# A scan's scaled old states no longer count in the estimate that places its next matmuls

## The chip, the cores and the metric

The kernel runs on one core of a Trainium2 chip. The core has five engines with queues of their own, each worked off strictly in the order in which the program was written: TensorE (PE, matmuls), VectorE (DVE), ScalarE (ACT), GpSimd (POOL) and SyncE (SP, which only issues DMAs; ACT issues some too). The metric is the device time of one execution in microseconds (us), the median of several runs. Lower is better.

## The reference

One encoder layer is applied to two request groups with one set of weights: group 0 has 512 tokens, group 1 has 1024. The kernel treats them as three blocks of 512 (b = 0 and 1 belong to group 1, b = 2 to group 0).

```python
x = x + 0.5 * mod[2] * rmsnorm(swiglu(h, f1_w1, f1_w3, f1_w2), n1_post)   # feed-forward 1
z = modulate(rmsnorm(x, nm_pre), ...) @ w_in                               # projections
m = concat([pool_mixer(z[..., :512]), rwkv7_mixer(token_shift(z[..., 512:]))])
x = x + mod[5] * rmsnorm(m @ w_out, nm_post)
x = x + 0.5 * mod[8] * rmsnorm(swiglu(h, f2_w1, f2_w3, f2_w2), n2_post)   # feed-forward 2
# in rwkv7_mixer, for each of 8 heads and both directions, token by token:
S = S * w_t + (S @ na_t) b_t^T + v_t k_t^T
y = S @ r_t
```

## The kernel before, in words

**Two kinds of work on PE.** The feed-forwards and projections are matmuls of 128x128 by 128x512 on split operands (each product is three of them: high by high, low by high, high by low). They are called wide matmuls here; there are 11520, written in a fixed sequence, and "wide matmul 6384" is the 6384th of them. They write the tiles u, v and y from hh, hl, gh, gl (split activations) and whi, wlo (split weights; whi is an ACT copy, wlo a subtraction on POOL or, while the scan runs, on DVE). All other matmuls are narrow; most belong to the scan.

**The scan.** The recurrence is done in chunks of 64 tokens. Eight pairs of heads (four of group 1, then four of group 0), each with all chunks in groups of four, give 24 groups and 96 steps. For a group, `scan_prep` loads and builds the operands (AR, BKt, MU), `scan_inv` inverts a triangular matrix per chunk (tile XN; even groups on DVE, odd ones on POOL; one inversion at a time), `scan_state` makes the four steps, and `scan_post` normalises the output (tile yT) and stores it to DRAM (m). A step of `scan_state` has two directions and these stages:

1. W: matmuls from the old state SBD and from MU into PSUM (tile sb), copied by ACT to a piece of XN (`wsb`, so the trace shows XN<-sb);
2. ACT scales the old states by a decay into s0p, two instructions per step, left out at the first and the last step of a pair (160 in all);
3. U: matmuls of XN and MU, copied by ACT (MU<-sb);
4. matmuls with BKt for the new state and with AR for the output, and on DVE the new state SBD <- sb, PL, s0p.

**What sets the order.** All parts are Python generators. While the program is written, `run_until` always continues one of them, and so decides which instructions come next in every engine's queue. It does so by an estimate: `Estimate.op` adds up assumed costs per engine, and keeps in `est.last` when the latest result written since a generator was continued would be there. At `yield WAIT` the generator becomes ready again at that time plus a lead (200 ns for the scan's steps, which have priority 0):

```python
elif r == CHAIN:
    p_.ready = est.last - CHAIN_LEAD
else:
    p_.ready = max(est.last + (AFTER_STATE if p_.prio == 0 else AFTER_OTHER), est.free["T"] + (0.0 if r == WAIT else r))
```

Until then the other generators, the main program (`mainC`) above all, put their matmuls into PE's queue. None of this is a wait on the chip; there, PE takes its queue in order, and each instruction waits for its own operands by semaphores.

**The main program around the scan** runs, in wide matmuls: feed-forward 1 of block 2 (up to 5712), pooled half of the output projection for block 0 (to 5808), the projections z of group 0 (to 6288), the pooled half for block 1 (to 6384), the other half for block 0, `wout_gen(0)` (to 6480), which needs the scan's output of all of group 1 and loads it with `mload_gen`, the pooled half for block 2 (to 6576), then feed-forward 2. The projections of group 0 begin with a norm of block 2, and feed-forward 2 of block 0 with a norm of what `wout_gen(0)` gave. A stretch in which no wide matmul stands because the main program cannot go on is called a hole here.

## Time and profile before

| what | value |
|---|---|
| median of 3 runs | 3704.02 us (3702.42 to 3704.77) |
| the profiled execution: its time | 3696.6 us |
| its span, first to last instruction | 3694.9 us |
| mean granted PE clock | 0.957 |
| PE, DVE, ACT, POOL busy | 94%, 54%, 39%, 38% of the span |
| first and last U matmul of the scan | 1258.4 and 2617.2 us |

A row of the page or of a view names line, engine, operation and tiles as out<-in. Every instruction of this kernel is recorded at one helper line (L161), so tiles tell what it is: sb and XN, MU, s0p, SBD belong to the scan's steps, sM to its other parts. A group has its count, its busy time in us and the mean in ns; a row of waits has the total in us, the times and the longest; a row of a timeline has start and length in us and, in brackets, the idle time before it and what ended it; a row of windows has length, then busy time (and instructions) of PE, weight load, DVE, ACT and POOL, the granted clock, the DMA share and GB/s.

### The profile page before, as it was taken

What the parts mean: (1) busy time and instruction counts of PE and PEld (TensorE: products, weight loads), DVE (VectorE), ACT (ScalarE), POOL (GpSimd) and SP (SyncE); (2) the same over time, 40 slices, a digit from 0 to 9 for tenths busy, and PEclk for the clock granted to TensorE, in tenths of its full rate; (3) what the DMA queues carried; (4) which work ended last, traced back from release to release, by engine and by line L of the source; (5) the groups of instructions that cost most, each with busy time, mean ns of one, the idle gap of its engine ahead of it and who ended that gap; (6) DMA issues with size and microseconds to landing.
All of it is one profiled execution on the core that took longest, in us unless ns stands there. A gap on an engine that the chain in (4) does not pass through costs nothing. (4 is left out here: it accounts for less than half of the span.)

```text
span 3694.9 us, 53680 instructions
## 1 busy us (share of the span) xinstructions
PE 3489.5 (94%) x19579; PEld 2639.9 (71%) x19579; DVE 2009.6 (54%) x3813; ACT 1436.3 (39%) x2776; POOL 1408.9 (38%) x1705
## 2 busy tenths in 40 slices
PE   7999999998999999999889989899999999999998
PEld 4667878886677666666666666567777788877886
DVE  3118272227326878777886888877467612241224
ACT  3324252224344444444444444543333432233222
POOL 2433444443123322333433234433354344444444
PEclk8999999998999999999978988799999999999999
DMA  7656353334334323223333344222354433343332
GB/s 280 221 182 185 99 151 91 98 92 125 121 123 138 92 82 92 69 78 95 109 100 102 113 144 126 81 86 72 109 177 129 117 100 95 94 123 117 99 91 79
DMA packets 557979, 432.10 MB, mean 117 GB/s; under 512 B 27029, under 2 KB 511572, under 8 KB 553620
## 3 DMA queue, kind: packets, MB, share of 16 engines
q1 hardware_dynamic: 524900, 379.90, 33.6%
q10 hardware_dynamic: 32816, 48.78, 4.2%
q8 instruction: 154, 2.52, 0.3%
q14 instruction: 109, 0.89, 0.1%
HBM read 367.23 MB, written 61.34 MB: 116 GB/s over the span
## 5 line engine op out<-in xcount | busy, mean ns | idle before, releaser
L161 POOL TENSOR_TENSOR wlo<-wraw,whi 128x512 fp32r<-128x512 f32 x670 | 888.0, 1343 | 1294.3 <-ACT whi L161 794.8
L161 DVE TENSOR_TENSOR y<-y,y 128x512 f32<-128x512 f32 x480 | 328.1, 685 | 866.2 <-PE y L161 865.0
L161 ACT ACTIVATE whi<-wraw 128x512 fp32r<-128x512 f32 x938 | 559.0, 622 | 186.3 <-PE v L161 141.5
L161 PE MATMUL u<-hh,whi 128*128 128x512 f32 x1392 | 567.5, 408 | 17.7 <-ACT hh L161 8.5
L161 PE MATMUL u<-hl,whi 128*128 128x512 f32 x1392 | 564.6, 406 | 14.1 <-DVE hl L161 14.0
L161 PE MATMUL v<-hh,whi 128*128 128x512 f32 x1392 | 562.8, 404 | 10.5 <-ACT hh L161 5.5
L161 PE MATMUL u<-hh,wlo 128*128 128x512 f32 x1392 | 566.4, 407 | 0.9 <-DVE wlo L161 0.6
L161 PE MATMUL v<-hl,whi 128*128 128x512 f32 x1392 | 563.0, 404 | 1.7 <-DVE hl L161 1.0
L161 PE MATMUL v<-hh,wlo 128*128 128x512 f32 x1392 | 561.6, 403 | 0.0
L161 PE MATMUL y<-gh,whi 128*128 128x512 f32 x1056 | 425.5, 403 | 12.3 <-DVE y L161 11.3
L161 PE MATMUL y<-gh,wlo 128*128 128x512 f32 x1056 | 422.2, 400 | 0.4 <-DVE wlo L161 0.4
L161 PE MATMUL y<-gl,whi 128*128 128x512 f32 x1056 | 422.5, 400 | 0.0
L161 POOL TENSOR_TENSOR XN<-XN 64x126 f32<-64x126 f32 (+22 forms) x744 | 335.3, 451 | 210.6 <-DVE XN L161 109.1
L161 PEld LDWEIGHTS u<-hh,whi 128*128 128x128 f32 x1392 | 266.3, 191 | 90.2 <-ACT hh L161 12.9
L161 PEld LDWEIGHTS u<-hl,whi 128*128 128x128 f32 x1392 | 266.5, 191 | 82.1 <-DVE hl L161 20.7
L161 ACT ACTIVATE gh<-s 128x512 fp32r<-128x512 f32 x132 | 83.3, 631 | 613.8 <-DVE s L161 613.4
L161 PEld LDWEIGHTS v<-hh,whi 128*128 128x128 f32 x1392 | 265.2, 191 | 79.1 <-ACT hh L161 9.4
L161 PEld LDWEIGHTS u<-hh,wlo 128*128 128x128 f32 x1392 | 266.9, 192 | 71.4 <-issue 10.9
L161 PEld LDWEIGHTS v<-hl,whi 128*128 128x128 f32 x1392 | 265.3, 191 | 68.9 <-issue 5.4
L161 PEld LDWEIGHTS v<-hh,wlo 128*128 128x128 f32 x1392 | 265.4, 191 | 63.5 <-issue 6.2
L161 PEld LDWEIGHTS y<-gh,whi 128*128 128x128 f32 x1056 | 200.9, 190 | 66.2 <-DVE y L161 14.8
L161 PEld LDWEIGHTS y<-gh,wlo 128*128 128x128 f32 x1056 | 200.7, 190 | 48.7 <-issue 3.2
(252 smaller groups left out, 4303.8 us busy)
## 6 DMA issues: line engine op xcount, KB each, us to landing
wraw<-in_f_w_dram SPq DMA_DIRECT2D x792, 256.0 KB
ada<-in_ada_w_dram SPq DMA_DIRECT2D x32, 1024.0 KB
wraw<-in_w_in_dram SPq DMA_DIRECT2D x98, 256.0 KB
xk<-xs ACTq DMA_DIRECT2D x96, 256.0 KB
xs<-y ACTq DMA_DIRECT2D x48, 256.0 KB
wraw<-in_w_out_dram SPq DMA_DIRECT2D x48, 256.0 KB
in_k<-zk SPq DMA_DIRECT2D x48, 128.0 KB
in_kk<-zkk SPq DMA_DIRECT2D x48, 128.0 KB
```

The costliest lines, as they stand in the source:

```text
L161: return f(*args, **kw)
```

## The change

`est.last` is saved before the two scalings of the old states and put back after them. The scalings are still issued, at the same place in ACT's queue, and their assumed cost still counts for ACT; only the time at which the step's generator becomes ready again no longer includes them.

```diff
                 for d in both:
                     S.activation(wsb[d], Wp[d], AF.Copy)
                 if not zero and not lastc:
+                    last = est.last
                     for d in both:
                         s0p[d] = st_(sb, [P, P], f"s0p{d}")
                         S.activation(s0p[d], old[:, d, :], AF.Copy, scale=PL[:, m % 2, gi, d, c:c + 1])
+                    est.last = last
                 yield WAIT
                 for h in both:
                     for d in both:
                         mm(Up[d][:, hl_(h)], MA[0:64, us(d, h), :], wsb[d][:, hl_(h)])
```

Every decision after the first such step can come out differently, so the whole order behind it is another one. The counts of PE's matmuls and of the DMAs are the same; 20 of the weights' low halves (wlo) go from DVE to POOL, since the scan ends earlier in the sequence. Its last matmul stands behind wide matmul 7214 before, and behind 6973 now.

PE at the second step of the scan that has scalings: from the end of W (sb<-MU) to U (sb<-XN,MU). Before:

```order
L161 MATMUL sb_9082<-MU_9075 64x64
L161 MATMUL y_9967<-gh_9576,wlo_9862 128x512
L161 MATMUL v_9928<-hh_8856,whi_9860 128x512
L161 MATMUL v_9928<-hl_8857,whi_9860 128x512
L161 MATMUL v_9928<-hh_8856,wlo_9924 128x512
L161 MATMUL v_9928<-hh_8856,whi_9860 128x512
L161 MATMUL v_9928<-hl_8857,whi_9860 128x512
L161 MATMUL v_9928<-hh_8856,wlo_9924 128x512
L161 MATMUL v_9928<-hh_8856,whi_9860 128x512
L161 MATMUL sb_9081<-XN_9076,MU_9075 64x64
L161 MATMUL sb_9082<-XN_9076,MU_9075 64x64
```

And with the change:

```order
L161 MATMUL sb_9082<-MU_9075 64x64
L161 MATMUL y_9967<-gh_9576,wlo_9862 128x512
L161 MATMUL v_9928<-hh_8856,whi_9860 128x512
L161 MATMUL v_9928<-hl_8857,whi_9860 128x512
L161 MATMUL v_9928<-hh_8856,wlo_9924 128x512
L161 MATMUL sb_9081<-XN_9076,MU_9075 64x64
L161 MATMUL sb_9082<-XN_9076,MU_9075 64x64
```

U stands four wide matmuls earlier.

SP around the end of the pooled half for block 1: wp_181 are its eight stores, one per column, m_177 and m_178 are the scan's last output of group 1 (from yT), and y<-wp opens `wout_gen(0)`. Before:

```order
L161 DMA wp_181<-gh_19272 128x512
L161 DMA wraw_19279<-in_w_out_dram 128x4x128
L161 DMA in_wa_19299<-zw_163 64x256 x2
L161 DMA in_wa_19299<-za_164 64x256 x2
L161 DMA in_k_19304<-zk_160 128x256 x2
L161 DMA in_kk_19307<-zkk_162 128x256 x2
L161 DMA in_r_19310<-zr_159 128x256 x2
L161 DMA wp_181<-gl_19346 128x512
L161 DMA m_177<-yT_17219 128x256
L161 DMA m_178<-yT_17219 128x256
L161 DMA y_19538<-wp_180 128x512 x8
```

And with the change (the eight wp_181 stores follow, and then y<-wp):

```order
L161 DMA m_179<-s_19149 128x512
L161 DMA m_177<-yT_17040 128x256
L161 DMA m_178<-yT_17040 128x256
L161 DMA wraw_19211<-in_w_out_dram 128x4x128
L161 DMA m_179<-s_19243 128x512
L161 DMA m_179<-s_19361 128x512
L161 DMA wp_181<-gh_19377 128x512
L161 DMA wraw_19384<-in_w_out_dram 128x4x128
L161 DMA wp_181<-gl_19452 128x512
```

The last store of the scan's group 1 stands behind the eighth column's store before, and ahead of the first one's now.

## The prediction

> **What bounds the kernel now.** I read the page first: its engine shares and its slices.

> ```profile
> span 3694.9 us, 53680 instructions
> PE 3489.5 (94%) x19579; PEld 2639.9 (71%) x19579; DVE 2009.6 (54%) x3813; ACT 1436.3 (39%) x2776; POOL 1408.9 (38%) x1705
> PE   7999999998999999999889989899999999999998
> PEclk8999999998999999999978988799999999999999
> ```

> The two rows of digits are 40 equal slices of 92 us: TensorE (PE) is busy nearly everywhere, and its granted clock sags in the second half of the scan (slices 21 to 26), where its busy share sags too. The chain of waits on the page does not reach back to the scan, so stages have to be compared by windows: the scan's first part, the middle, its end, and all that follows it.

> ```profile
> 1204.00:1815.00 611.00, 575.84 (x4410) 415.69 (x4409) 485.93 (x1083) 267.45 (x591) 186.23 (x364) 0.96 0.28 84
> 1815.00:2380.00 565.00, 504.42 (x3682) 355.22 (x3679) 449.24 (x994) 267.08 (x589) 230.97 (x415) 0.85 0.38 117
> 2380.00:2622.00 242.00, 232.88 (x1918) 169.18 (x1917) 172.60 (x391) 105.28 (x245) 69.03 (x140) 0.99 0.25 74
> 2622.00:3695.00 1073.00, 1033.34 (x4535) 834.23 (x4533) 415.93 (x609) 357.79 (x627) 477.70 (x362) 0.99 0.38 112
> ```

> Columns: length, then busy time of PE, weight load, DVE, ACT, POOL, then granted clock. I call lost the idle time of PE plus its busy time times (1 - clock): 58 us in the first part, 136 in the middle, 11 at the end, 50 in the 1073 us after the scan. So PE bounds, and the only stage with much to win or lose is the middle of the scan. What PE waits for, over the whole span:

> ```profile
> PE sM L161 <- DVE MU L161: 37.1, 23, 4.2
> PE sb L161 <- DVE SBD L161: 18.6, 32, 2.2
> ...
> PE sb L161 <- ACT XN L161: 1.9, 4, 1.0
> ```

> The last row is the one that the change touches: U matmuls (sb<-XN,MU) waiting for ACT's copies of W (XN<-sb) cost 1.9 us in all. The next step's W waits on the state (SBD), and the inverse's matmuls on DVE (MU), cost more, and the change leaves both alone.

> **The change part by part.** No instruction is added or removed on PE; 160 scalings stay on ACT where they were, behind the two copies. Only places move: PE's U matmuls come forward. One step of the scan in the trace:

> ```profile
> 1710.16 0.45 PE L161 MATMUL sb<-MU 64*64 64x64 f32 x8
> 1710.54 0.50 PE L161 MATMUL y<-gh,whi 128*128 128x512 f32 x1
> 1710.68 0.57 ACT L161 ACTIVATE XN<-sb 64x128 f32<-64x128 f32 x2 [0.78 <-ACT Pt L161]
> 1711.15 0.68 ACT L161 ACTIVATE s0p<-SBD,PL 128x128 f32<-128x128 f32 x2
> 1712.71 0.39 PE L161 MATMUL v<-hh,whi 128*128 128x512 f32 x1
> 1713.03 0.45 PE L161 MATMUL sb<-XN,MU 64*64 64x64 f32 x8
> 3252.28 5.60 PE v L161 x24
> ```

> The copies end at 1711.25 and U starts at 1713.03: 1.78 us in which PE is never idle, because wide matmuls of the main program fill it. A wide matmul takes 5.60/24 = 0.233 us (last row, from the chain after the scan). In the order the commonest number of wide matmuls between W and U falls from 8 to 4, and over 96 steps from 674 to 431. The 243 are not saved, they run elsewhere: 0.233 x 243 = 57 us of cover that the scan no longer uses. **By itself that is 0 us**, since PE does the same work. The rest of the sum is what happens to lost time.

> *(1) The wait for the scan at the first output projection goes: -9 us.* The wide matmuls stop dead for 24 us at number 6384, and the trace says why:

> ```profile
> 2194.95 0.39 PE L161 MATMUL u<-hh,wlo 128*128 128x512 f32 x1
> 2202.18 1.91 PE L161 MATMUL sM<-MU 32*32 32x32 f32 x32 [2.19 <-DVE MU L161]
> 2207.95 1.27 POOL L161 TENSOR_TENSOR yT<-yT,pg 128x512 f32<-128x512 f32 x1
> 2209.25 0.80 SPq L161 DMA_DIRECT2D m<-yT  x2
> 2210.86 0.33 ACTq L161 DMA_DIRECT2D xk<-m  x1
> 2218.54 0.61 ACT L161 ACTIVATE hh<-xk 128x512 fp32r<-128x512 f32 x1
> 2219.21 0.79 PE L161 MATMUL u<-hh,whi 128*128 128x512 f32 x1 [0.23 <-ACT hh L161]
> 2195.00:2219.30 24.30, 18.34 (x183) 13.51 (x181) 16.05 (x34) 9.81 (x25) 9.79 (x23) 0.62 0.54 181
> 2219.30:2246.00 26.70, 26.15 (x160) 17.43 (x160) 17.36 (x34) 8.84 (x23) 22.18 (x45) 0.71 0.22 62
> ```

> The last piece of the scan's output for the first request group is only finished by POOL at 2209.22, stored, loaded back (xk), split (hh), and then the projection starts. In the new order that store lies eight projection columns earlier, so the scan is no longer what is waited for; the load itself still is, because it is requested only when the matmuls before it are written into the order: 2219.21 - 2210.86 = 8.4 us. Work in the hole at full clock is 18.34 x 0.62 = 11.4 us, so 12.9 are lost. Afterwards 34 of the 94 narrow matmuls stand there, 11.4 x 34/94 = 4.1 us, so 8.4 - 4.1 = 4.3 are lost. Difference 8.6, taken as 9. Bounds: -13 (nothing lost) to 0 (another wait takes its place).

> *(2) The slow clock behind that hole: -2 us.* The row 2219.30:2246.00 loses 26.15 x 0.29 = 7.6 us. Shorter holes are followed by a slow clock too (the 8.2 us hole below stands at 0.74), so I take a quarter. Bounds -8 to 0. [...]

> *(3) U waits for the copies: +5 us.* With 4 wide matmuls U would start about 1 us after W, and ACT's copies need 0.71 us (1710.54 to 1711.25): 0.2 to 0.3 us of margin. ACT is busy (267.45 + 267.08 + 105.28)/1418 = 45% of the scan, mostly with pieces like this:

> ```profile
> L161 ACT ACTIVATE whi<-wraw 128x512 fp32r<-128x512 f32 x938 | 559.0, 622 | 186.3 <-PE v L161 141.5
> L161 ACT ACTIVATE s0p<-SBD,PL x160: 385/390/403, 1267.7 to 2610.1; 128x128 f32<-128x128 f32 x160
> ```

> A copy that comes behind one is late by 0 to 0.62 us evenly; less 0.2 of margin that is 0.42 x 0.42/(2 x 0.62) = 0.14 us on average, times 0.45, times the 80 steps that have scalings: 5 us. Behind U on PE stand wide matmuls, which then wait for nothing but lose that time. Bounds: 0 to 80 x 4 x 0.233 = 75 us (each step loses all that it gained), and the first is far nearer, as 1.9 us are lost now. The scalings take 0.39 us each and end at 1711.83 in the step above, before the copies of U are wanted at about 1712.5, so they move no wait.

> *(4) Scan work moves into the second set of projections: -6 us.* Between wide matmuls 5808 and 6288 the order holds 20 U steps where it held 16, and the 251 wide matmuls up to the scan's old end (6963 to 7214) hold one U step where there were nine. Those projections wait for their own finishing work:

> ```profile
> 1874.30:2135.30 261.00, 243.42 (x1721) 170.59 (x1722) 194.94 (x448) 125.83 (x274) 87.65 (x184) 0.88 0.33 98
> 2135.30:2143.50 8.20, 4.05 (x50) 3.16 (x48) 7.56 (x21) 1.83 (x4) 0.70 (x1) 0.74 0.80 243
> ```

> Here 261.0 - 243.4 = 17.6 us are idle, and moved work can fill some of that. I take a third. Bounds -18 to 0.

> *(5) Norms crowded on DVE: +3 us.* From the first to the eighth scaling of the norm that the next feed-forward waits for (at 6576), DVE has 62 instructions in the new order against 27, since an inversion now falls there.

> ```profile
> 2301.10:2339.20 38.10, 28.18 (x251) 22.19 (x249) 32.39 (x68) 16.41 (x37) 10.77 (x8) 0.62 0.41 134
> 2339.15 0.80 PE L161 MATMUL u<-hh,whi 128*128 128x512 f32 x1 [4.03 <-ACT hh L161]
> L161 DVE TENSOR_TENSOR XN<-XN x744: 156/256/1419, 1209.5 to 2529.6; 64x126 f32<-64x126 f32 x18, 64x30 f32<-64x30 f32 x12, 64x56 f32<-64x56 f32 x12, 64x78 f32<-64x78 f32 x12
> 1864.20:1874.30 10.10, 4.30 (x51) 3.43 (x49) 8.55 (x25) 2.73 (x5) 1.95 (x5) 0.77 0.54 156
> ```

> DVE is 32.39/38.10 = 85% busy in that hole, so instructions put there count: 35 x 0.256 = 9 us. Against it the norm before this one is broadcast at wide matmul 6501 instead of 6528: 27 x 0.233 = 6 us earlier. Net +3. The hole at 5808 (last row) gets more of both, waits and work, and I leave it at 0. Bounds 0 to +18 with both holes.

> Sum: -9 - 2 + 5 - 6 + 3 = -9 us. The profiled execution took 3696.6 us (span 3694.9), so 3688 for it; it lay 7 us under the median of 3704.0, against which I forecast **3695**.

> **The rivals.** *Nothing is left (3704).* The hole at 6384 keeps its length because another wait takes over, and the filled idle time returns elsewhere. For it: in the scan's first part, step 40 stands at wide matmul 5711 instead of 5722, that is, the inverses and not the steps set the pace there. Against it: the store visibly moves.

> *Slower: the inversion sits in front of the norm (3718).* Its place is the hole at 6576: DVE does the 35 extra instructions (9 us) before the norm is through, nothing comes earlier for it, and the first 24 wide matmuls behind it run at half clock (24 x 0.233 = 6 us more); the hole at 5808, which must hold 78 narrow matmuls instead of 28, grows by 50 x 11.4/94 = 6 us. That is 21 on top of the sum without (5), -12: +9, and with (3) twice as large +14. It decides from the point where the hole at 6576 is over 50 us long. For it: the 85% of DVE. Against: less scan work of PE stands in that hole, 58 narrow matmuls instead of 132.

> *A larger gain (3681).* (1) and (2) at their far bounds and (4) at -10: -13 - 8 + 5 - 10 + 3 = -23. For it: the middle of the scan loses 136 us, and removing one hole may spare a slow clock that follows it. Against: four other holes stay.

> *Short waits lower the clock (3721).* If 80 short waits more take the scan's clock down by 0.02, that is 1313 us of PE busy time x 0.02 = 26 us on top of the forecast. [...]

> **How the numbers follow.** A measurement of this kernel tells about 0.2%, 7.4 us, from no change, so faster means under 3696.6 and slower over 3711.4. Chances: forecast 0.36 (3689 to 3700; 0.28 of it under the bound), nothing left 0.22, larger gain 0.17, norm slower 0.18, clock 0.07. Faster 0.28 + 0.17 = 0.45; within 0.08 + 0.22 = 0.30; slower 0.18 + 0.07 = 0.25. Range 3671 to 3721: down to -33, near the sum of the far bounds of (1), (2) and (4) with (3) and (5) as taken (-13 - 8 - 18 + 5 + 3 = -31), up to +17, which takes in the norm case. The forecast's own range is 3689 to 3700.

> **What would show it.** (1): between the wide matmuls 6384 and 6385 no more than 12 us, begun by the load xk and not by the store m<-yT. (3): the wait of sb on ACT XN rises from 1.9 us to 4 to 10. (4): idle in the second projections under 17 us. (5): the hole at 6576 between 35 and 48 us. The last U of the scan near 2560 us instead of 2617. The prediction is wrong if the hole at 6384 keeps 20 us or more, if waits on XN pass 15 us, or if the clock in the scan's first part falls under 0.94.

## The result and the profile after

The changed kernel takes 3717.6 us (median of 6 runs, 3712.7 to 3731.2) against 3701.8 us of the kernel before on the same chip. The ratio is **1.0051, with an interval of 1.0035 to 1.0067**: slower by half a per cent, 16 us by the two medians and 19 us by the ratio. The forecast was 3695, a small gain; the measured time is inside the range and on the other side of no change.

The page of the kernel after, its span, the row of PE, and the slices of PE and of its granted clock:

```profile
span 3723.8 us, 53718 instructions
PE 3518.8 (94%) x19579; PEld 2664.9 (72%) x19579; DVE 1988.0 (53%) x3789; ACT 1434.3 (39%) x2774; POOL 1431.2 (38%) x1729
PE   7999999998999999999889989799999999999998
PEclk8999999998999989999969888799999999999999
```

The profiled execution took 3725.65 us, 8 us over its median, and the one before 3696.6 us, 5 us under its own; so the two profiles lie some 13 us further apart than the medians. Span less busy time gives PE's idle time: 3723.8 - 3518.8 = 205.0 us, and 3694.9 - 3489.5 = 205.4 before. **PE waits no longer than before.** The same 19579 matmuls are busy for 29.3 us more, and the span is 28.9 us longer. So the whole difference of the two profiles is a slower clock: the clock records hold 402.6 us at half clock, against 318.6 before.

The four windows of the prediction, in the kernel after (the last one ends with its span):

```profile
1204.00:1815.00 611.00, 581.56 (x4368) 420.99 (x4367) 475.07 (x1075) 265.10 (x587) 181.78 (x362) 0.93 0.28 83
1815.00:2380.00 565.00, 505.15 (x3771) 354.81 (x3769) 447.18 (x997) 258.93 (x587) 227.79 (x418) 0.84 0.37 115
2380.00:2622.00 242.00, 225.74 (x1743) 163.84 (x1742) 165.76 (x381) 107.79 (x240) 86.15 (x152) 0.91 0.25 74
2622.00:3722.00 1100.00, 1062.90 (x4659) 859.18 (x4657) 414.03 (x599) 363.69 (x636) 490.78 (x374) 0.99 0.37 111
```

The clock went from 0.96, 0.85 and 0.99 to 0.93, 0.84 and 0.91 in the first three of these windows; behind the scan nothing changed. And PE's longest waits in the scan:

```profile
PE sM L161 <- DVE MU L161: 25.1, 19, 3.6
PE sb L161 <- DVE SBD L161: 18.8, 26, 2.3
PE sb L161 <- ACT XN L161: 12.7, 9, 5.2
```

U waits 10.8 us more for ACT's copies, the inverse's matmuls 12.0 us less for DVE: one against the other.

Windows with fixed times compare different work here, so the next rows go by the work itself: from wide matmul 5712 to 5808, to 6288, to 6384, to 6576 and to 7214. Before:

```profile
1815.90:1874.30 58.40, 48.58 (x379) 34.49 (x377) 53.77 (x109) 30.36 (x68) 40.20 (x70) 0.96 0.56 176
1874.30:2143.50 269.20, 247.47 (x1770) 173.75 (x1770) 202.50 (x468) 127.66 (x278) 88.35 (x184) 0.87 0.35 103
2143.50:2219.20 75.70, 67.30 (x518) 46.68 (x518) 61.66 (x145) 35.05 (x84) 23.57 (x35) 0.77 0.46 145
2219.20:2339.20 120.00, 106.58 (x805) 77.40 (x805) 99.08 (x225) 51.39 (x119) 45.13 (x63) 0.81 0.38 118
2339.20:2621.80 282.60, 266.27 (x2099) 191.04 (x2099) 203.94 (x440) 127.73 (x287) 102.75 (x205) 0.95 0.25 73
```

The same stages after:

```profile
1824.70:1893.80 69.10, 58.62 (x454) 42.79 (x452) 59.28 (x128) 32.66 (x75) 42.34 (x71) 0.85 0.48 153
1893.80:2194.00 300.20, 276.83 (x2016) 196.35 (x2016) 228.91 (x554) 137.16 (x307) 94.45 (x193) 0.83 0.33 97
2194.00:2264.30 70.30, 61.35 (x456) 40.24 (x456) 54.13 (x105) 33.70 (x80) 41.57 (x75) 0.79 0.45 145
2264.30:2397.40 133.10, 111.78 (x851) 78.20 (x849) 109.82 (x251) 55.05 (x128) 49.50 (x79) 0.82 0.35 111
2397.40:2653.00 255.60, 243.61 (x1778) 179.91 (x1779) 163.92 (x349) 114.07 (x247) 99.06 (x161) 0.94 0.28 85
```

"Lost" is, as in the prediction, idle time of PE plus busy time times (1 - clock):

| stage (wide matmuls) | U steps | us | lost us |
|---|---|---|---|
| 5712 to 5808 | 4, now 3 | 58.4, now 69.1 | 11.8, now 19.3 |
| 5808 to 6288, second projections | 16, now 20 | 269.2, now 300.2 | 53.9, now 70.4 |
| 6288 to 6384, with the hole of term (1) | 4, now 5 | 75.7, now 70.3 | 23.9, now 21.8 |
| 6384 to 6576, with the hole of term (5) | 8, now 8 | 120.0, now 133.1 | 33.7, now 41.4 |
| 6576 to 7214 | 24, now 19 | 282.6, now 255.6 | 29.6, now 26.6 |

The work moved forward as the order said, and the end of the scan gave 27 us back. But the stages that took it in grew by 49 us, so this stretch is 22.4 us longer. The clearest places of the kernel after are these windows: the hole at 5808 and the 45 us behind it, the hole at 6072 and the 37 us behind it, the hole at 6384 and the 27 us behind it, and the hole at 6576.

```profile
1869.00:1893.80 24.80, 17.67 (x151) 12.96 (x150) 20.90 (x56) 10.47 (x23) 6.26 (x7) 0.58 0.31 99
1893.80:1938.60 44.80, 37.18 (x256) 25.57 (x257) 38.20 (x103) 23.08 (x47) 15.14 (x12) 0.61 0.18 50
2052.40:2063.10 10.70, 8.68 (x99) 7.33 (x97) 9.17 (x26) 3.27 (x6) 0.00 (x0) 0.72 0.12 35
2063.10:2100.00 36.90, 36.90 (x236) 25.95 (x235) 23.48 (x45) 18.61 (x44) 18.24 (x43) 0.71 0.34 102
2254.30:2264.30 10.00, 7.36 (x70) 4.80 (x68) 8.53 (x26) 4.05 (x12) 2.79 (x4) 0.71 0.91 328
2264.30:2291.00 26.70, 24.17 (x139) 15.11 (x138) 20.13 (x57) 8.49 (x21) 4.92 (x4) 0.66 0.28 85
2371.50:2397.40 25.90, 15.06 (x115) 10.40 (x113) 21.95 (x71) 8.55 (x23) 3.34 (x4) 0.56 0.15 52
```

The prediction shows the three holes before, and the window behind the one at 6384. The windows of the kernel before behind the places 5808 and 6072, of the same lengths, are:

```profile
1874.30:1919.10 44.80, 40.35 (x228) 26.45 (x229) 38.58 (x86) 26.23 (x55) 13.42 (x16) 0.60 0.13 36
2028.00:2064.90 36.90, 35.08 (x271) 25.62 (x270) 33.34 (x97) 17.41 (x42) 3.36 (x12) 1.00 0.38 112
```

Behind 5808 the clock was as slow before (0.60 and 0.61). At 6072 the change is large: the hole and the window behind it lose 4.5 + 10.7 = 15.2 us, and the same place before loses 1.8.

The hole at 6072 is new: 0.2 us before (no narrow matmul stands there in that order), 10.7 us with 52 of them now. The timeline of the kernel after shows the main things queued in it:

```profile
2051.85 2.16 DVE L161 STREAM_TRANSPOSE MU<-XN 32x512 f32<-32x512 f32 x2
2054.10 1.05 PE L161 MATMUL y<-bones,acc 128*128 128x2 f32 x8 [1.32 <-ACT acc L161]
2055.09 1.19 PE L161 MATMUL sM<-MU 32*32 32x32 f32 x32
2056.08 0.17 DVE L161 TENSOR_SCALAR ms<-y 128x8 f32<-128x8 f32 x1
2059.68 1.28 DVE L161 TENSOR_TENSOR MU<-sM,mask 128x512 f32<-128x512 f32 x2
2060.51 1.88 PE L161 MATMUL sM<-MU 32*32 32x32 f32 x32 [0.35 <-DVE MU L161]
2060.88 0.68 DVE L161 TENSOR_TENSOR gl<-gl,y 128x512 f32<-128x512 f32 x1
2063.09 0.78 PE L161 MATMUL v<-hh,whi 128*128 128x512 f32 x1
```

The projection's norm (acc, ms, gl) and the scan's next group, the end of its inversion (XN, MU, sM) and the building of operands, take turns on DVE and PE, each behind the other in the queues, and the next wide matmul comes only after both. Behind the hole PE is never idle (36.90 of 36.90 us), and still the mean clock there is 0.71: the records hold one stretch at half clock from 2057.1 to 2084.4 us.

### The profile page after: what moved, and what is told of

Same layout as the page of the kernel before. It is cut to its first block, busy times and chain, and to the rows that moved or that the text cites. A ratio compares the mean times of both kernels' runs of the same rounds, so it can differ in the third digit from the quotient of the medians.

```text
span 3723.8 us, 53718 instructions
## 1 busy us (share of the span) xinstructions
PE 3518.8 (94%) x19579; PEld 2664.9 (72%) x19579; DVE 1988.0 (53%) x3789; ACT 1434.3 (39%) x2774; POOL 1431.2 (38%) x1729
## 5 line engine op out<-in xcount | busy, mean ns | idle before, releaser
L161 POOL TENSOR_TENSOR wlo<-wraw,whi 128x512 fp32r<-128x512 f32 x690 | 913.6, 1342 | 1323.2 <-ACT whi L161 884.8
L161 DVE TENSOR_TENSOR y<-y,y 128x512 f32<-128x512 f32 x480 | 328.2, 685 | 882.2 <-PE y L161 881.4
L161 ACT ACTIVATE whi<-wraw 128x512 fp32r<-128x512 f32 x938 | 559.0, 622 | 193.0 <-PE v L161 149.6
L161 PE MATMUL u<-hh,whi 128*128 128x512 f32 x1392 | 569.2, 409 | 14.7 <-ACT hh L161 5.1
L161 PE MATMUL u<-hl,whi 128*128 128x512 f32 x1392 | 567.0, 407 | 13.2 <-DVE hl L161 11.8
L161 PE MATMUL v<-hh,whi 128*128 128x512 f32 x1392 | 569.0, 409 | 9.1 <-ACT hh L161 4.8
L161 PE MATMUL v<-hl,whi 128*128 128x512 f32 x1392 | 567.5, 408 | 6.1 <-POOL hl L161 3.6
L161 PE MATMUL u<-hh,wlo 128*128 128x512 f32 x1392 | 568.0, 408 | 0.1
L161 PE MATMUL v<-hh,wlo 128*128 128x512 f32 x1392 | 567.6, 408 | 0.0
L161 PE MATMUL y<-gh,whi 128*128 128x512 f32 x1056 | 424.4, 402 | 7.7 <-DVE y L161 6.7
L161 PE MATMUL y<-gh,wlo 128*128 128x512 f32 x1056 | 423.4, 401 | 0.4 <-DVE wlo L161 0.4
L161 PE MATMUL y<-gl,whi 128*128 128x512 f32 x1056 | 422.9, 400 | 0.0
L161 POOL TENSOR_TENSOR XN<-XN 64x126 f32<-64x126 f32 (+22 forms) x744 | 327.5, 440 | 204.2 <-DVE XN L161 59.8
L161 ACT ACTIVATE gh<-s 128x512 fp32r<-128x512 f32 x132 | 83.3, 631 | 661.8 <-DVE s L161 661.8
L161 PEld LDWEIGHTS u<-hh,whi 128*128 128x128 f32 x1392 | 268.3, 193 | 85.1 <-ACT hh L161 8.6
L161 PEld LDWEIGHTS u<-hl,whi 128*128 128x128 f32 x1392 | 268.1, 193 | 82.7 <-DVE hl L161 17.0
L161 PEld LDWEIGHTS v<-hh,whi 128*128 128x128 f32 x1392 | 268.6, 193 | 77.2 <-ACT hh L161 7.6
L161 PEld LDWEIGHTS v<-hl,whi 128*128 128x128 f32 x1392 | 269.0, 193 | 72.9 <-POOL hl L161 5.5
L161 PEld LDWEIGHTS u<-hh,wlo 128*128 128x128 f32 x1392 | 268.1, 193 | 68.1 <-issue 9.2
L161 PEld LDWEIGHTS v<-hh,wlo 128*128 128x128 f32 x1392 | 268.7, 193 | 65.3 <-issue 6.5
L161 PEld LDWEIGHTS y<-gh,whi 128*128 128x128 f32 x1056 | 200.7, 190 | 60.3 <-DVE y L161 9.1
L161 PEld LDWEIGHTS y<-gh,wlo 128*128 128x128 f32 x1056 | 200.8, 190 | 48.2 <-issue 2.6
```

What stands on the lines that cost most here:

```text
L161: return f(*args, **kw)
```

## The experiments

**Where the change applies.** In `part1` it holds for the first 40 steps of the scan only, in `part2` only for the rest (m is the pair of heads).

```diff
-                    est.last = last
+                    if m < 5:      # part2: m >= 5
+                        est.last = last
```

> The change only in the first 40 of 96 steps (macro steps m under 5); later scalings count in the estimate again. Clock theory: the scan's first stage (wide matmuls 4473 to 5712) takes about 568 us as in the changed kernel against 558 before, then about as before: 3702 to 3717. Norm theory: as the kernel before if the hole at 5808 is about 10 us long, +15 to +25 us if it is about 25. Order theory: anywhere from -20 to +20 us, and not where the change acts.

Measured: 1.0039 (1.0026 to 1.0053); wait of U for XN 5.8 us, hole at 5808 30.2 us, half clock 380.1 us.

> The change only from step 41 on (m of 5 and more). The order is the old one up to there. Clock theory: first stage 558 us as before, and the middle (wide matmuls 5712 to 6700) 10 to 30 us longer with more half clock: 3705 to 3725. Norm theory: follows the lengths of the holes at 5808 and 6576. Order theory: anywhere from -20 to +20 us.

Measured: 1.0054 (1.0040 to 1.0069); wait for XN 2.0 us, hole at 5808 16.8 us, half clock 349.4 us. Each half alone costs as much as the whole, and the second half costs it with no more waiting for the copies than before (1.9). So the cost is not a sum of small prices of early U's.

**Filling the holes.** In `before_fill` and `after_fill` PE gets an extra wide matmul on a constant, whose result nothing reads, about every 500 ns of estimated time in which the main program is stuck during the scan: 76 and 77 of them. `filled` marks such waits of the main program.

```diff
+    def fill():
+        if stuck and est.free["T"] >= filled_at[0] + 500.0:
+            filled_at[0] = est.free["T"]
+            nc.tensor.matmul(pm.tile([P, TB], F32, name=nm("fill"), tag=stuck[0], bufs=1),
+                             idr[:, 0:1].to_broadcast([P, P]), idr[:, 0:1].to_broadcast([P, TB]),
+                             start=True, stop=True, skip_group_check=True)
```

> The kernel before, in its own order, with 76 wide matmuls added that nobody reads, placed only where the main program is stuck in a hole of the scan (18 us of TensorE work at full clock). Clock theory (half clock follows stretches of about 3.4 us with fewer than 4 wide matmuls): more work, less time; half-clock time falls from 319 us to about 220, time 15 to 40 us under the kernel before. Norm theory (holes are waits for DVE): half-clock time may fall, but the holes keep their length, time 0 to +18 us. Order theory (any reordering of the scan moves the time by some tens of us by chance): says 0 to +18 us too, as the order is kept.

Measured: 1.0034 (1.0019 to 1.0050), half clock 300.7 us instead of 318.6 (220 by the clock theory), PE idle 190.4 us instead of 205.4. What the clock theory goes by, in the scan of the kernel before: of the pieces of 3.41 us at full clock, 18 of 29 in which up to 3 wide matmuls begin are followed by half clock, and none of the 318 others.

> The changed kernel, in its own order, with 77 unread wide matmuls in the holes of the scan. Clock theory: half-clock time falls from 403 us to about 270, time 25 to 50 us under the changed kernel, so 3670 to 3695, and at most 15 us over before_fill. Norm theory: the hole at wide matmul 5808 stays at 25 us or more, time 3718 to 3735. Order theory: 3718 to 3735.

Measured: 1.0085 (1.0072 to 1.0099), half clock 362.1 us instead of 402.6 (270 by the clock theory), PE idle 192.3 instead of 205.0. The extra work (77 x 0.233 = 18 us) costs more than it gives. That it raises the clock is not shown: of the 40 us less half clock in `after_fill`, 37 lie between the wide matmuls 4473 and 5712 (47.8 us against 85.3), where only one extra matmul stands. So it is not enough to fill the empty places of a hole; that the scan's matmuls there come later when something stands in front is likely, and no run took it apart.

**Other orders by the same rule.** The lead after a step (`AFTER_STATE` in the code quoted above) is turned by 5 to 20 ns, with and without the change. The work is the same, and so, nearly, is the distance between W and U: 635 to 674 wide matmuls over the 96 steps without the change, 421 to 469 with it. Only the planner's decisions fall otherwise. All twelve kernels differ in this line alone, from the kernel before or from the changed one:

```diff
-AFTER_STATE = 200
+AFTER_STATE = 190    # and 180, 185, 205, 210, 220
```

> The kernel before with the lead of the scan's steps at 190 ns instead of 200: U still has 8 wide matmuls of cover most often (661 in all against 674), but the whole order comes out anew (the scan ends at wide matmul 7173 instead of 7214). Cover theory (time is lost because U has half the cover): like the kernel before, ratio 0.999 to 1.002. Order theory (the kernel before has a lucky order, and any new order of the scan costs): 1.003 to 1.006, as in the two partial changes.

> The kernel before with a lead of 210 ns: 668 wide matmuls of cover, scan ends at 7173. Cover theory: ratio 0.999 to 1.002. Order theory: 1.003 to 1.006.

> The changed kernel with a lead of 190 ns: U has 4 wide matmuls of cover most often (433 in all against 431), but the scan ends at 7128 instead of 6973. Cover theory: like the changed kernel, ratio 1.003 to 1.007. Order theory: anywhere from 0.998 to 1.006, on average the same as the two kernels before with another lead.

> The changed kernel with a lead of 210 ns: 422 wide matmuls of cover, scan ends at 7155. Cover theory: ratio 1.003 to 1.007. Order theory: 0.998 to 1.006, no different on average from the kernels before with another lead.

> The kernel before with a lead of 180 ns: 635 wide matmuls of cover, 8 most often, another order. Order theory: a further draw from the same spread as before, before_lead190 and before_lead210 (3702 to 3736). Cover theory: 3698 to 3706.

> The changed kernel with a lead of 180 ns: 469 wide matmuls of cover, 4 most often, an order that shares much with after_lead190. Order theory: a further draw from the spread of the changed kernels (3690 to 3718), and half-clock time tells where in it: 0.33 us per us of half clock. Cover theory: 3712 to 3725.

> The estimate without the change, the constant for the time after a state at 185 instead of 200; cover between W and U 655 wide matmuls (674 at 200). The measured ratio to the kernel before is a draw of the order in one theory: then this kernel lies between 1.000 and 1.010, as the four orders without the change did (1.0000, 1.0093, 1.0036, 1.0051). In the other theory the kernel before is typical of its kind and the two slow ones were outliers: 1.000 +- 0.002.

> The change with the constant at 185; cover 457. If the order draws the time and the change is worth what the forecast said, this lies between 0.996 and 1.005 and under its partner without the change in most of the pairs, by 0.36% on average over all. If U placed early costs the 0.5% that was measured, it lies over its partner by about 0.5%.

> Without the change, constant at 205; cover 674 as in the kernel before. Same cover, another order: by the draw anywhere from 1.000 to 1.010; by the other theory 1.000 +- 0.002.

> The change with the constant at 205; cover 431 as in the changed kernel, steps with no cover 14 as there. By the draw anywhere from 0.996 to 1.005; if the steps without cover are what costs, 1.005 +- 0.002 as in the changed kernel, which has the same 14.

> Without the change, constant at 220; cover 661. By the draw anywhere from 1.000 to 1.010; by the theory that the kernel before is typical, 1.000 +- 0.002.

> The change with the constant at 220; cover 421. By the draw anywhere from 0.996 to 1.005 and, over the seven pairs, under its partner on average; if U placed early costs, over its partner by about 0.5%.

Measured, as ratios to the kernel before on the same chip (intervals are +-0.0008 to 0.0023), with the length of the stretch from wide matmul 5712 to 7214 in the profile:

| lead, ns | without the change | stretch, us | with the change | stretch, us |
|---|---|---|---|---|
| 180 | 1.0051 | 821.9 | 0.9998 | 809.2 |
| 185 | 1.0050 | 825.2 | 0.9980 | 810.5 |
| 190 | 1.0093 | 842.5 | **0.9968** | 806.2 |
| 200 | 1 | 805.9 | 1.0051 | 828.4 |
| 205 | 0.9994 | 805.8 | 1.0069 | 830.3 |
| 210 | 1.0036 | 816.8 | 1.0020 | 821.0 |
| 220 | 1.0007 | 810.4 | 1.0005 | 814.2 |

Four things follow.

First, 10 ns of an assumed lead move this kernel by up to 0.9%, as much as anything that the change does. The kernel with the change and a lead of 190 takes 3689.9 us and beats both kernels (0.9957 to 0.9979); without the change the same lead is the slowest of all.

Second, it is the order and not chance from run to run. The orders at 200 and 205 are near twins: by the tile names in the traces they differ at only 73 of 19579 places on PE without the change and at 61 with it (the kernels before and after differ at 8267), and they give nearly the same ratios and the same stretch. The rows of the stretch, first two without the change (at 205 and at 190), then two with it (at 205 and at 190), each from its own kernel's windows:

```profile
1819.40:2625.30 805.90, 736.44 (x5571) 523.28 (x5567) 620.94 (x1382) 372.34 (x832) 299.87 (x555) 0.89 0.34 104
```

```profile
1824.10:2666.70 842.60, 758.53 (x5580) 540.90 (x5579) 627.50 (x1392) 374.89 (x835) 294.65 (x561) 0.86 0.33 99
```

```profile
1811.60:2641.90 830.30, 749.89 (x5551) 535.09 (x5550) 616.88 (x1384) 372.50 (x834) 326.88 (x579) 0.86 0.34 104
```

```profile
1815.00:2621.20 806.20, 733.84 (x5551) 525.17 (x5550) 624.91 (x1389) 367.23 (x821) 303.33 (x558) 0.89 0.35 105
```

The clock in it is 0.89 in the two quick orders and 0.86 in the two slow ones. Over the 16 orders, with the two halves of the change, stretch and ratio go together (correlation 0.94; 1 us of the stretch is 1.1 us of the median).

Third, what U's early place is worth by itself stays open. The seven differences, with less without the change, are -0.53, -0.70, -1.25, +0.51, +0.75, -0.16 and -0.02%: mean -0.20 +- 0.26% (standard error), and since neighbouring leads can give nearly one order they hold less than seven independent draws. The forecast's gain (-9 us, -0.24%) is as possible as nothing; a general cost of 0.5%, which the one measured pair suggests, lies 2.7 such errors away.

Fourth, the new order's weakest place can be named by comparison, but it is no rule for other orders. In the stage of the second projections, the kernel with the change and a lead of 190 reads

```profile
1882.70:2151.60 268.90, 243.40 (x1843) 171.71 (x1841) 216.11 (x519) 132.04 (x294) 87.24 (x191) 0.91 0.34 102
```

It holds 19 U steps in 268.9 us, where the kernel before has 16 in 269.2 and the changed kernel 20 in 300.2. Its hole at 6072 is 3.6 us with 10 narrow matmuls instead of 10.7 us with 52, for there the norm's part on DVE is through before the wide matmuls run out. The near twin at 205 has the hole again, 11.0 us. Behind it the clock in the twin is 0.91 and not 0.71:

```profile
2047.60:2084.50 36.90, 36.09 (x273) 25.74 (x271) 26.49 (x52) 20.94 (x52) 20.45 (x44) 0.91 0.38 116
```

So one and the same hole can be followed by a fast or a slow clock, and the twin is slow all the same. Other orders are slow without this hole: it is 1.4 us long in `part1`, 4.7 us in `part2` and 0.2 us in `before_lead190`, the slowest of all. And the quickest, the change with a lead of 190, has the longer hole at 5808, 29.2 us against 24.8. No run moved a hole alone; what makes an order slow stays open.

**What a stop costs.** To find the price of a single short stop of PE, `pause1` puts one round trip (PE to DVE to PE, on data that nothing reads) ahead of each of 22 up-projections of feed-forward 2 of block 1, behind the scan, where the clock stood at 0.99; `pause4` puts four in a row there.

```diff
+        def pause():
+            if which == 2 and b == 1:
+                for i in range(1 + 1):      # pause4: 4 + 1
+                    pz = ps.tile([P, TB], F32, name=nm("hop"), tag="s0", bufs=1)
+                    nc.tensor.matmul(pz[:, 0:2], ident, scr if i else bones2, start=True, stop=True,
+                                     skip_group_check=True)
+                    if i < 1:               # pause4: 4
+                        nc.vector.tensor_copy(scr, pz[:, 0:2])
         def uv(f, down=None):
+            pause()
```

> The kernel before with one short pause of TensorE ahead of each of the 22 up-projections of the last but one feed-forward, behind the scan, where TensorE otherwise has no idle time: a small matmul, a DVE copy of its result, a small matmul of that. Idle-window theory (a 3.4 us window with 1.5 us or more of idle time halves the clock, and only a window with almost none brings it back): about 0.6 to 0.9 us idle each, no half clock, so 13 to 20 us longer and half-clock time unchanged at 319 us within 20.

Measured: 1.0295 (1.0279 to 1.0310), +110 us, 5.0 us for each place, where 13 to 20 us in all were expected. What the theory goes by, in the scan of the kernel before: of the pieces of 3.41 us at full clock, 11 of 16 with 1.5 us or more of idle time are followed by half clock, and 7 of 331 with less; of those at half clock, 17 of 36 without idle time are followed by full clock, and 1 of 32 with some.

> The same with four such hops in a row, 2.4 to 3.6 us idle at each of 22 places. Idle-window theory: each place halves the clock for one or two windows (3.4 to 6.8 us), so half-clock time rises by 75 to 150 us and the kernel is longer by four times the extra time of pause1 (52 to 80 us) plus another 25 to 70 us. If the clock does not follow idle windows: four times pause1 and no more.

Measured: 1.0414 (1.0397 to 1.0431), +154 us; the three further trips cost 44/66 = 0.66 us each. The first place in the timeline of `pause1`:

```profile
2919.89 0.28 PE L892 MATMUL hop<-bones,ident 128*128 128x2 f32 x2
2920.80 1.77 DVE L161 TENSOR_TENSOR hl<-sq,hh 128x512 fp32r<-128x512 f32 x1
2923.69 0.15 DVE L895 COPY scr<-hop 128x2 f32<-128x2 f32 x1
2923.89 0.59 PE L892 MATMUL hop<-scr,ident 128*128 128x2 f32 x2 [3.72 <-DVE scr L895]
2924.34 0.78 PE L161 MATMUL u<-hh,whi 128*128 128x512 f32 x1
```

the windows of that stop and of the 10 us behind it,

```profile
2919.90:2923.90 4.00, 0.28 (x4) 0.19 (x2) 3.84 (x6) 1.50 (x4) 1.26 (x1) 0.99 0.32 92
2923.90:2934.00 10.10, 10.10 (x42) 8.40 (x43) 3.88 (x12) 3.17 (x6) 1.67 (x2) 0.84 0.39 117
```

and the groups of the second hop, of `pause1` and of `pause4` (matmuls | busy, mean ns | idle before):

```profile
L892 PE MATMUL hop<-scr,ident 128*128 128x2 f32 x44 | 10.3, 304 | 57.8 <-DVE scr L895 57.8
```

```profile
L892 PE MATMUL hop<-scr,ident 128*128 128x2 f32 x176 | 43.8, 319 | 74.4 <-DVE scr L895 74.4
```

The copy takes 0.15 us, but it stands on DVE behind four large instructions; so one trip idles PE for 57.8/22 = 2.6 us. Then the clock falls, to 0.84 in the 10.10 us behind it, though PE has no idle time there: half-clock time is 420.4 us instead of 318.6, that is 4.6 us for each stop. In sum 58 us idle, 16 us of hops (10.3 and 6.1) and 102 us at half clock; at the 0.37 us that one such us costs (the fit under (2) in the next section) that is 58 + 16 + 37 = 111, and the span is 111.4 us longer. In `pause4` the 66 extra trips add only 16.6 us of idle time, 0.25 us each, against 2.6 us for a first one. **In `pause1` a stop cost the queue that it stood behind, 2.6 us, and then a slow clock, 4.6 us at half clock**; its own work, 16 of the 111 us, counted least.

## Why the prediction was wrong, point by point

*What bounds.* Right: PE, and the middle of the scan is where time is won or lost.

*By itself 0 us.* It held for waiting: 205.4 and 205.0 us of idle time, with 243 wide matmuls less between W and U.

*(1) The wait for the scan at 6384.* Right. The hole is 10.0 us instead of 24.3 and loses 2.6 + 7.36 x 0.29 = 4.8 us instead of 12.9: -8.1, forecast -8.6, taken as -9. It is begun by the load and not by the store, as the timeline of the kernel after shows (ACT requests xk when the wide matmuls have run out):

```profile
2254.33 0.39 PE L161 MATMUL u<-hh,wlo 128*128 128x512 f32 x1
2254.82 0.33 ACTq L161 DMA_DIRECT2D xk<-m  x1
2262.12 0.62 ACT L161 ACTIVATE hh<-xk 128x512 fp32r<-128x512 f32 x1
2264.32 0.80 PE L161 MATMUL u<-hh,whi 128*128 128x512 f32 x1
```

*(3) U waits for the copies.* Right in kind: 12.7 us instead of 1.9, so +10.8 where +5 was taken; the wait is a little past the 4 to 10 named.

*(5) The norms on DVE.* Half wrong. The hole at 6576 shrank to 25.9 us (35 to 48 forecast). The hole at 5808, "left at 0", grew from 10.1 to 24.8 us; its own loss went from 6.8 to 14.6 us. The window behind it lost 22.1 us, but 20.6 before, so little of that is new.

***(4), the step that failed.*** The sum took -6 for scan work that moves into the second projections: idle time there would be filled. It was not. The idle time is 23.4 us instead of 21.7 and the stage's loss rose by 16.5 us, 13.4 of them at the new hole at 6072 and behind it. In the twins at 205, rows below, the loss rises too, from 53.7 to 63.3 us, and the idle time from 21.5 to 25.7.

```profile
1877.80:2146.90 269.10, 247.58 (x1770) 173.73 (x1770) 202.52 (x468) 127.76 (x278) 88.21 (x184) 0.87 0.34 103
1880.80:2175.00 294.20, 268.48 (x2016) 190.40 (x2016) 228.53 (x554) 136.88 (x307) 94.71 (x193) 0.86 0.33 99
```

Even where the stage gains, it does not gain by filling: with a lead of 190 it loses 25.5 + 243.4 x 0.09 = 47.4 us with three more U steps, 6.5 less than in the kernel before, but its idle time is higher (25.5) and only its clock is better (0.91 against 0.87). The forecast looked at the holes that the old order had and not at those that the new one makes, where an inversion falls beside a norm.

***(2), the term that was mis-sized.*** The slow clock got -2 us, for the one hole that shortens, and nothing anywhere else. (The 8.2 us row that the prediction cites for it gives the clock in a hole and not behind one; in the 16.5 us behind that hole it was 0.51.) Even there it went the other way: the window of 26.7 us behind the hole stood at 0.71 before and stands at 0.66 now. Over the span it is 84 us more at half clock. A fit over the profiles of the 16 orders gives span = 3415 + 0.80 x idle + 0.37 x half-clock time, with 2.5 us of scatter; so 84 us are 31 us, all of the 29 us between the two profiles. Some of this is not the order's: from wide matmul 4473, where the scan begins, to 5712 the profile of the kernel after is 9.0 us longer than before (567.6 against 558.6). `part1` repeats that (567.6), but the near twin at 205 and `after_fill`, with the same order there, show 553.5 and 553.0. The 22 us of the stretch behind it come back in the twin.

*The rivals.* "Short waits lower the clock (3721)" has the size (the first part's clock fell by 0.03, under the 0.94 named as a sign of error), but not the mechanism. Its 0.02 was an assumption, and no run shows it apart; over 1204 to 2622 us the clock went from 0.92 to 0.89. In the near twin at 205, with the same order from wide matmul 4473 to 5712, the clock there is 0.96 and not 0.92, and `after_lead180` and `after_lead190` have nearly as little cover between W and U and wait 9.3 and 10.0 us for the copies, and they are not slower. "The inversion sits in front of the norm (3718)" had a picture that fits, an inversion and a norm in one queue, at the wrong hole: 6072 and 5808, not 6576. "A larger gain" is near what the lead of 190 gave (0.9968, 3690). The last U came at 2590 us, between 2560 and the old 2617.

## What to carry to other kernels

Where a planner sets the order, one measured pair tells about one draw: perturb a constant that should not matter, with and without the change, before a difference under 1% is given to the change. Look through the new order, and not only the old one, for places where two chains meet in one queue and no large work is left in front: in the changed kernel the largest new loss of its profile stands at such a place, though other orders were slow without it. Take a second profile, of a near twin, before a slow clock at one place is given to the order. Price a stop of TensorE as the queue it waits behind plus the slow clock that follows (2.6 us, and 4.6 us at half clock, in `pause1`), and look at the clock before the idle time when the busy time grows.

## What the runs showed of the hardware that was not expected

**It rose late where narrow matmuls were mixed in, idle time or not.** From half clock, 1 of 329 windows with 0.5 us or more of idle time is followed by full clock, and 10 of 177 with some, but less. Without any idle time (by the profile, which models where a matmul ends) it goes with the number of matmuls begun in the window: up to 9 (nearly all wide), 122 of 123 are followed by full clock; 10 to 25, 203 of 424; 26 and more, 3 of 145. Counted by wide matmuls, with idle time or without, it is 96 of 96 with 7 or more, 150 of 324 with 4 to 6, and 93 of 778 with fewer. So the wide work in a window tells the clock about as well as idle time does, and no run separates the two. The half clock behind the hole at 6072, with PE busy all the time, fits: the windows from 2063.9 us begin 28, 20, 23, 18, 16 and 8 matmuls, and full clock follows the last.

**Half clock cost 0.37 us per us here, not 0.5**, an estimate by the fit above (0.02 standard error); 0.5 would be the loss if all of PE's work took twice as long. Why it is less was not shown. So the "lost" of the prediction and of the table above, which counts 0.5, overstates the clock's share.
